# A two-layer diffusion step: feed-forward borders with weight splits behind the first half's tiles, a fixed order of the first seven-product blocks, and the output weights' splits one piece ahead

## The chip, the core and the metric

The kernel runs on one core of a Trainium2 chip. The core has five engines that run their own instruction streams: TensorE (PE, matrix products), VectorE (DVE), ScalarE (ACT), GpSimd (POOL) and SyncE (SP, which here issues nearly all transfers). They wait for each other on semaphores only. The metric is the device time of one execution in microseconds (us).

## The reference

The program is one inference step of a two-layer backbone for 128 prompt tokens and 512 sample tokens, both of width 1024. The kernel treats them together as 640 columns, in two halves of 320. Every layer is a mixer (attention) and a feed-forward part; each part is modulated by shift, scale and gate vectors that come from a conditioning vector. The feed-forward part, to which the change belongs, computes

```
h   = rms_norm(x, norm_ffn) * (1 + scale2) + shift2
g, u = split(h @ w_ffn_in)              # 1024 -> 2 x 2816
x   = x + gate2 * ((silu(g) * u) @ w_ffn_out)   # 2816 -> 1024
```

and `mods = silu(cond) @ w_mod + b_mod` gives the shifts, scales and gates of every layer.

## The kernel before

**Arithmetic.** Products are made from a high and a low part of each fp32 operand: `hi = round(a)`, `lo = a - hi`, and three matmuls of 128 x 128 weights on 320 columns (hi x hi, hi x lo, lo x hi; `mm3`, all at L61 in the trace). For every weight tile there is thus a load from memory (SP), a high part (ACT, a Copy) and a low part (DVE, a subtraction), before TensorE can use it. `unit` makes such a tile (L162 load, L170 high, L171 low).

**Feed-forward, first stage.** The 2816 hidden features are 22 blocks of 128. Blocks 0 and 1 are plain (`eight`): for each of eight input tiles k, three matmuls with the gate weight (`fg`) and three with the up weight (`fu`), for the left half of the columns (`fg_00`) and for the right half (`fg_01`). Blocks 2 to 21 use seven block products in the manner of Strassen (`product`, four tiles each, 12 matmuls): the input operands D, N, C, E and the pairs of `h01q` tiles are sums made once per layer by `add_up`; the weights X, Y, Z, W of each block are made from its raw gate and up weights `wg`, `wu` (class `Weights`): four sums on DVE (`s`, written `s13` and `s24` in the source), then a high part (`hi`, ACT) and a low part (`lo`, DVE) of each. A block's products come as X, D (with weight Y), N (with Z), the second X, Z, C (with Y), and E (with W) one block later. `job` is the block before, whose E product, gate and hidden value are finished during the present one. For blocks 2 and 3 the two X products are made ahead (`ahead`), among the plain blocks. Names: `h01q` are the input tiles of layer 0 (`h11q` in layer 1), `wgu` a plain block's weights, `wX`, `wY`, `wZ`, `wW` the others, `fd` the bank of D and Z, `fg` that of X, N, C and E.

**The border before it.** The first half's norm and the input tiles come out of the mixer's output stage: `oanacc` sums the squares of the eight output tiles (L205 on DVE; `ocnacc` in layer 1), two matmuls with ones (`oanp`) make the second half's row sums while the first tiles of block 0 run, and `make` writes each input tile's high and low part: for the left half, even k on DVE (L293 and L294), odd k on POOL (L290 and L291); for the right half, high on ACT and low on DVE (L287, L288).

**Second stage.** The output product has eight output tiles n and the 22 hidden blocks, taken in two passes: FIRST (9 blocks), SECOND (13 blocks). Hidden blocks that were written to memory (`sp`) are read back as `hr` (function `again`, helper `some`). `wout` loads a piece of the output weights and splits it (`wo_0_45`: pass 0, output tile 4, from block 5 on; L1329 on ACT, L1330 on DVE). Each output bank (`fo_...`) is added to the residual `xr` by DVE (L313).

**Side work.** The modulation of the next part is made on DVE during this: `step` loads weight tiles `wm` and multiplies them with `silu(cond)`, held in `cb` (`junk`, L1418, two operations of 128 x 1024 for each tile). Two Silu operations on ACT prepare `cb` (L1422).

**What sets the order.** The code is written per operation, and a scheduler puts the instructions of each engine in an order from its own costs and the dependences; each engine then runs its list strictly in order. `after(inst, fn)` forces what `fn` issues behind `inst` on the same engine; class `Line` chains the operations of one stream (`dve`, `act`) in the order in which they are written. Buffers rotate: `rawp` holds three raw weight tiles for all loads by `load`, so that a load waits until the third tile before it is used up. SP issues transfers in order, and a transfer that waits holds up those behind it.

## Time and profile before

| what | value |
|---|---|
| time, median of three runs (range) | 1534.39 us (1533.13 to 1541.67) |
| the profiled execution: its time, its span | 1534.34 us, 1532.5 us |
| TensorE busy, share of the span | 1465.5 us, 96% |
| DVE, ACT, POOL busy | 1143.5 us (75%), 738.4 us (48%), 230.2 us (15%) |
| granted TensorE clock | 0.994 |
| layer 0: first matmul of blocks 0 and 1, of block 2, of the output product, of layer 1 | 394.73, 433.36, 674.72, 834.29 us |
| layer 1: first matmul of blocks 0 and 1, of block 2, of the output product | 1083.32, 1121.92, 1364.51 us |

A timeline row has the start in us, the duration, the engine, the line, the operation, what it writes and reads, and in brackets how long the engine sat idle before it and which engine's work ended that wait. A row of windows has the busy time and the number of instructions (x) of an engine in a stretch. The span is what lies between the first and the last instruction; 1.8 us of the time lie around it. A matmul's duration reads longer than the step to the next one, since matmuls overlap.

### The profile page before, as it was taken

What the parts mean: (1) busy time and instruction counts of PE and PEld (TensorE: products, weight loads), DVE (VectorE), ACT (ScalarE), POOL (GpSimd) and SP (SyncE); (2) the same over time, 40 slices, a digit from 0 to 9 for tenths busy, and PEclk for the clock granted to TensorE, in tenths of its full rate; (3) what the DMA queues carried; (4) which work ended last, traced back from release to release, by engine and by line L of the source; (5) the groups of instructions that cost most, each with busy time, mean ns of one, the idle gap of its engine ahead of it and who ended that gap; (6) DMA issues with size and microseconds to landing.
All of it is one profiled execution on the core that took longest, in us unless ns stands there. A gap on an engine that the chain in (4) does not pass through costs nothing.

```text
span 1532.5 us, 25615 instructions
## 1 busy us (share of the span) xinstructions
PE 1465.5 (96%) x9928; PEld 1409.3 (92%) x9928; DVE 1143.5 (75%) x2115; ACT 738.4 (48%) x1447; POOL 230.2 (15%) x303
## 2 busy tenths in 40 slices
PE   5999989989999999999999899999999999999997
PEld 4889878879999999999999889989989999999997
DVE  5646687875889999957998787765888997743333
ACT  5445577763655444431224556663655444441221
POOL 0215635522100000000002433212100000000000
PEclk9999999999999999999999999999999999999999
DMA  9324541005155555578773210003154555367211
GB/s 370 112 95 170 170 141 39 18 21 172 43 189 176 177 180 190 174 261 307 232 227 120 90 41 29 28 15 110 42 190 162 176 181 159 128 233 251 85 41 69
DMA packets 73674, 215.09 MB, mean 140 GB/s; under 512 B 8160, under 2 KB 13040, under 8 KB 73296
## 3 DMA queue, kind: packets, MB, share of 16 engines
q1 hardware_dynamic: 71504, 210.09, 41.3%
q10 hardware_dynamic: 1632, 2.43, 0.5%
q8 instruction: 78, 1.28, 0.3%
q0 software_dynamic: 416, 0.93, 0.2%
q14 instruction: 44, 0.36, 0.1%
HBM read 184.96 MB, written 28.46 MB: 139 GB/s over the span
## 4 chain that ended last, share of the span: by engine, by line
PE 80%; DVE 10%; ACT 5%; DMA 2%; issue 2%; POOL 0%; POOLq 0%; DVEq 0%; SPq 0%; ACTq 0%
PE fg L61 18%; PE fo L61 10%; PE fd L61 9%; PE fu L61 5%; PE gq L61 2%; PE nk L61 2%; PE nq L61 2%; PE go L61 1%; PE fo_4b L61 1%; PE fo_2b L61 1%; PE fo_0b L61 1%; PE fo_0a L61 1%; PE fo_4a L61 1%; PE fo_2a L61 1%; PE fo_6a L61 1%
## 5 line engine op out<-in xcount | busy, mean ns | idle before, releaser
L1078 ACT ACTIVATE sg<-g 128x320 f32<-128x320 f32 x40 | 18.9, 472 | 154.2 <-DVE g L1078 154.2
L1418 DVE SCALAR_TENSOR_TENSOR junk<-wm,cb 128x1024 bf16<-128x1024 f32 x62 | 75.6, 1220 | 3.2 <-DMA wm<-in_wm 2.4
L245 POOL TENSOR_SCALAR h10h<-h10t,gs,mods 128x320 fp32r<-128x320 f32 x4 | 3.6, 892 | 426.4 <-DVE h10t L239 424.7
L61 PE MATMUL gq<-h10h,wgq 128*128 128x320 f32 x256 | 65.6, 315 | 0.2
L1078 DVE SCALAR_TENSOR_TENSOR junk<-wm,cb 128x1024 bf16<-128x1024 f32 x50 | 61.0, 1220 | 0.8
L1078 DVE TENSOR_TENSOR wZ<-s,wZ 128x1024 fp32r<-128x1024 f32 x40 | 48.7, 1218 | 0.8 <-ACT wZ L1078 0.8
L1078 DVE TENSOR_TENSOR wY<-s,wY 128x1024 fp32r<-128x1024 f32 x40 | 48.7, 1218 | 0.0
L61 PEld LDWEIGHTS gq<-h10h,wgq 128*128 128x128 f32 x256 | 44.7, 188 | 1.6 <-PE gtp L65 1.0
L1078 ACT ACTIVATE wY<-s 128x1024 fp32r<-128x1024 f32 x40 | 42.0, 1050 | 7.5 <-DVE s L1078 7.5
L1078 ACT ACTIVATE wZ<-s 128x1024 fp32r<-128x1024 f32 x40 | 42.4, 1061 | 1.5 <-DVE s L1078 1.5
L313 DVE SCALAR_TENSOR_TENSOR xr<-fo,mods,xr 128x320 f32<-128x320 f32 (+2 forms) x48 | 19.6, 435 | 29.8 <-PE fo L61 29.7
L1602 ACT ACTIVATE gp<-gs,gb,rq 128x640 f32<-128x640 f32 (+1 forms) x40 | 31.9, 798 | 19.7 <-DVE gb L1601 17.6
L61 PE MATMUL fg<-h11N,wZ 128*128 128x320 f32 x240 | 39.1, 310 | 1.9 <-ACT wZ L1078 1.2
L61 PE MATMUL fd<-h01D,wY 128*128 128x320 f32 x240 | 39.2, 309 | 1.5 <-ACT wY L1078 1.3
L61 PE MATMUL fd<-h11D,wY 128*128 128x320 f32 x240 | 39.2, 309 | 1.5 <-ACT wY L1078 1.3
L1078 DVE TENSOR_TENSOR sg<-up,sg 128x640 f32<-128x640 f32 (+1 forms) x40 | 31.4, 785 | 12.2 <-ACT sg L1078 12.2
L61 PE MATMUL fg<-h01N,wZ 128*128 128x320 f32 x240 | 38.9, 310 | 0.9 <-ACT wZ L1078 0.9
L61 PE MATMUL gq<-h10l,wgq 128*128 128x320 f32 x128 | 39.4, 308 | 0.0
L61 PE MATMUL fg<-h01q,wX 128*128 128x320 f32 x240 | 38.8, 309 | 0.0
L61 PE MATMUL fg<-h11q,wX 128*128 128x320 f32 x240 | 38.8, 309 | 0.0
L61 PE MATMUL fd<-h01q,wZ 128*128 128x320 f32 x240 | 38.6, 309 | 0.1
L61 PE MATMUL fd<-h11q,wZ 128*128 128x320 f32 x240 | 38.6, 309 | 0.0
(3024 smaller groups left out, 5323.3 us busy)
## 6 DMA issues: line engine op xcount, KB each, us to landing
wm<-in_wm SPq DMA_DIRECT2D x48, 512.0 KB, 3.6
mraw<-in_wm SPq DMA_DIRECT2D x24, 512.0 KB, 3.7
mraw<-in_wm SPq DMA_DIRECT2D x8, 1024.0 KB, 15.3
wm<-in_wm0g SPq DMA_DIRECT2D x8, 512.0 KB, 3.5
x<-in_xT SPq DMA_DIRECT2D x8, 320.0 KB, 5.5
xr<-in_xT SPq DMA_DIRECT2D x8, 320.0 KB, 5.6
cb<-in_crow SPq DMA_DIRECT2D x2, 1024.0 KB, 5.7
gt<-in_rpbp SPq DMA_DIRECT2D x8, 240.0 KB, 3.5
```

The costliest lines, as they stand in the source:

```text
L61: cls.last = nc.tensor.matmul(*a, **k)
L245: G.tensor_scalar(h[:, c0:c1], t, self.gsl[:, k, 0:1], self.ml[:, self.sh + k, 0:1], ALU.mult, ALU.add)
L313: V.scalar_tensor_tensor(xo[:, c0:c1], ps[:, c0 - o:c1 - o], ml[:, g + n, c:c + 1], xi[:, c0:c1], ALU.mult, ALU.add)
L1078: self.last = after(self.last, lambda: op(*a, **k))
L1418: def step(kind, at, line=lambda op, *a, **k: op(*a, **k)):
L1602: S.activation(dst, src, AF.Exp, bias=nb, scale=rq[:, j:j + 1], accum_out=ll[:, j:j + 1])
```

## The change

Three places are edited, in both layers.

**The border to block 0.** Tiles k = 5 and 7 of the left half are made by DVE and no longer by POOL (per layer four POOL operations less, four DVE operations more). The low parts of `wX_3` and of block 1's two weights `wgu_10`, `wgu_11` are forced behind the last tile's low part (`hm.done`; being a DVE instruction, this orders DVE alone). Block 1's raw weights no longer use the rotating `rawp` tiles, but the two tiles named "ws", which are free until the first block's sums; SP issues one of these loads ahead of the `xr` loads and one behind them in layer 0.

On DVE, at the end of the first half's norm, there stood before (`wX_3`, `wgu` low parts; `h01t` is x times the norm's factor; `xr_...` with `oanrs` a tile of the right half from `xr_4359` on):

```order
L205 TENSOR_TENSOR oanacc<-oanacc,oansq_4862 128x320
L171 TENSOR_TENSOR wX_3_5019<-wX_3r,wX_3_5019 128x1024
L293 CAST h01q_4751<-h0132d_4741 128x320
L205 TENSOR_TENSOR oanacc<-oanacc,oansq_4878 128x320
L294 TENSOR_TENSOR h01q_4751<-h0132d_4741,h01q_4751 128x320
L281 TENSOR_TENSOR h01t_4881<-xr_4696,oanrs 128x320
L171 TENSOR_TENSOR wgu_10_5024<-wgu_10r,wgu_10_5024 128x1024
L171 TENSOR_TENSOR wgu_11_5029<-wgu_11r,wgu_11_5029 128x1024
```

and there stands now:

```order
L208 TENSOR_TENSOR oanacc<-oanacc,oansq_4862 128x320
L297 TENSOR_TENSOR h01q_4750<-h0132a,h01q_4750 128x320
L284 TENSOR_TENSOR h01t_4865<-xr_4658,oanrs 128x320
L284 TENSOR_TENSOR h01t_4881<-xr_4696,oanrs 128x320
L208 TENSOR_TENSOR oanacc<-oanacc,oansq_4878 128x320
L296 CAST h01q_4751<-h0132d_4741 128x320
L297 TENSOR_TENSOR h01q_4751<-h0132d_4741,h01q_4751 128x320
L296 CAST h01q_4752<-h0132d_4741 128x320
L297 TENSOR_TENSOR h01q_4752<-h0132d_4741,h01q_4752 128x320
L180 TENSOR_TENSOR wX_3_5019<-wX_3r,wX_3_5019 128x1024
```

The low part of `wX_3` now follows the last sum of squares (`oansq_4878`) and the tiles k = 5 to 7, and the low parts of `wgu` have left this place (they follow nine and eleven rows later).

**The first seven-product blocks.** Block 2's raw weights are fetched and summed earlier, right behind the left half's gate of block 0; its parts are made as X, Y, Z and then W (W was first). For blocks 2 and 3 (`first`), the next block's weight parts are made behind the evacuation of N (`u1`) and not between the products, and every block's D product is forced behind the last matmul that was written before it. The Silu operations on `cb` move two blocks later, into the `act` chain.

On TensorE, at the border to the seven-product blocks, there stood before (the last three matmuls of N of block 2, and what follows; `h01D` and `h01N` are operands, the numbers tell tiles apart):

```order
L61 MATMUL fg_2_4988<-h01N_4772,wZ_2_5305 128x320 x3
L61 MATMUL fd_3_5394<-h01D_4761,wY_3_5326 128x320 x2
L61 MATMUL fg_3_5061<-h01N_4769,wZ_3_5327 128x320
L61 MATMUL fd_3_5394<-h01D_4761,wY_3_5326 128x320
L61 MATMUL fd_3_5394<-h01D_4762,wY_3_5326 128x320
L61 MATMUL fd_2_5314<-h01q_4757,wZ_2_5305 128x320 x3
L61 MATMUL fd_2_5314<-h01q_4758,wZ_2_5305 128x320 x3
L61 MATMUL fd_2_5314<-h01q_4759,wZ_2_5305 128x320 x3
L61 MATMUL fd_2_5314<-h01q_4760,wZ_2_5305 128x320 x3
L61 MATMUL fg_2_4988<-h01C_4765,wY_2_5304 128x320 x3
```

and there stands now:

```order
L61 MATMUL fg_2_4988<-h01N_4772,wZ_2_5046 128x320 x3
L61 MATMUL fd_2_5314<-h01q_4757,wZ_2_5046 128x320 x3
L61 MATMUL fd_2_5314<-h01q_4758,wZ_2_5046 128x320 x3
L61 MATMUL fd_2_5314<-h01q_4759,wZ_2_5046 128x320 x3
L61 MATMUL fd_2_5314<-h01q_4760,wZ_2_5046 128x320 x3
L61 MATMUL fg_2_4988<-h01C_4765,wY_2_5045 128x320 x3
L61 MATMUL fg_2_4988<-h01C_4766,wY_2_5045 128x320 x3
L61 MATMUL fg_2_4988<-h01C_4767,wY_2_5045 128x320 x3
L61 MATMUL fg_2_4988<-h01C_4768,wY_2_5045 128x320 x3
L61 MATMUL fd_3_5392<-h01D_4761,wY_3_5326 128x320 x3
```

Nothing of block 3 (`fd_3`, `fg_3`) stands ahead of block 2's Z and C products any more.

**The output weights.** In the first pass, `prepare(i + 1)` loads and splits the next piece ahead of the present piece's matmuls; the read-backs (`some`) begin with the third output tile. On DVE, around the split of output tile 5's first piece, there stood before:

```order
L313 SCALAR_TENSOR_TENSOR xr_4553<-fo_0_4a,mods_98,xr_4553 128x320
L1418 SCALAR_TENSOR_TENSOR junk_8354,mods_99<-wm_13_8346,cb 128x1024
L313 SCALAR_TENSOR_TENSOR xr_4553<-fo_0_4b,mods_98,xr_4553 128x192
L313 SCALAR_TENSOR_TENSOR xr_4553<-fo_0_4b,mods_98,xr_4553 128x128
L1330 TENSOR_TENSOR wo_0_50_8360<-wo_0_50r,wo_0_50_8360 128x640
L1330 TENSOR_TENSOR wo_0_55_8395<-wo_0_55r,wo_0_55_8395 128x512
```

and there stands now:

```order
L1346 TENSOR_TENSOR wo_0_45_8258<-wo_0_45r,wo_0_45_8258 128x512
L316 SCALAR_TENSOR_TENSOR xr_4419<-fo_0_2a,mods_98,xr_4419 128x320
L1346 TENSOR_TENSOR wo_0_50_8295<-wo_0_50r,wo_0_50_8295 128x640
L316 SCALAR_TENSOR_TENSOR xr_4419<-fo_0_2b,mods_98,xr_4419 128x192
L316 SCALAR_TENSOR_TENSOR xr_4419<-fo_0_2b,mods_98,xr_4419 128x128
L1443 SCALAR_TENSOR_TENSOR junk_8337,mods_99<-wm_12_8333,cb 128x1024
```

`wo_0_50` has moved ahead of the residual of output tile 2 from behind that of tile 4, past three modulation tiles (six `junk` operations); on SP its load moved with it.

The diff, cut to what does this (moved code that is unchanged is left out):

```diff
+    def unit(src, n, name, lo="v", pool=None, behind=None, raw=None):
+        if raw is None:
+            raw = load(src, n, name + "r")
+        else:
+            nc.sync.dma_start(raw, src)
...
-        S.activation(hi, raw, AF.Copy)
-        (V if lo == "v" else G).tensor_tensor(lw, raw, f(hi), ALU.subtract)
+        after(behind, lambda: S.activation(hi, raw, AF.Copy))
+        after(behind, lambda: (V if lo == "v" else G).tensor_tensor(lw, raw, f(hi), ALU.subtract))
...
-            elif k % 2:
+            elif k in (1, 3):
                 G.tensor_scalar(h, h32, 1.0, 0.0, ALU.mult, ALU.add)
                 G.tensor_tensor(l, h32, f(h), ALU.subtract)
             else:
                 V.tensor_copy(h, h32)
-                V.tensor_tensor(l, h32, f(h), ALU.subtract)
+                self.done = V.tensor_tensor(l, h32, f(h), ALU.subtract)
...
+        def fetch_g(fb):
+            if fb == FEW:
+                raws[fb].append(load(wFI[l, fb, 0], 1024, f"wg{l}_{fb}r"))
+            elif fb < FB:
...
+        done = hm.done
...
-        wX += [unit(wFI[l, FEW + i, 1], 1024, f"wX{l}_{FEW + i}") for i in range(1, AHEAD)]
-        w1 = [unit(wFI[l, 1, i], 1024, f"wgu{l}_1{i}") for i in range(2)]
+        wX += [unit(wFI[l, FEW + i, 1], 1024, f"wX{l}_{FEW + i}", behind=done) for i in range(1, AHEAD)]
+        w1 = [unit(wFI[l, 1, i], 1024, f"wgu{l}_1{i}", behind=done, raw=fp.tile([P, 1024], F32, tag="ws", bufs=2, name=f"wgu{l}_1{i}r"))
+              for i in range(2)]
+        fetch_u(FEW)
+        fetch_g(FEW)
+        w = Weights(FEW)
         sg = tmp(f"sg{l}_0")
         gated(sg, 0)
+        w.sums()
...
-        w.hi_w()
-        w.lo_w()
-        w.sums()
         for c in "XYZ":
             w.hi(c)
             w.lo(c)
+        w.hi_w()
+        w.lo_w()
...
+            first = fb < FEW + AHEAD
...
             if n:
                 n.sums()
+            if n and not first:
                 n.hi("X")
...
-            product(b5, w.Y, 0, "D", True)
+            after(PE.last, lambda: product(b5, w.Y, 0, "D", True))
...
             act(S.activation, u1, g[:, :HT], AF.Copy)
             if n:
+                if first:
+                    for c in "XYZ":
+                        n.hi(c)
+                        n.lo(c)
+                    fetch_u(fb + 2)
+                    n.hi_w()
                 n.lo_w()
                 fetch_g(fb + 2)
...
-            step("load", fb + 1)
+            step("load", fb + 1, act)
...
-        for n in range(KT):
-            plan = ((3, 6),) if n < 4 else ((0, 5), (5, 4))
...
+        jobs = [(n, j0, m) for n in range(KT) for j0, m in (((3, 6),) if n < 4 else ((0, 5), (5, 4)))]
+        ready = {}
+        def prepare(i):
+            if i < len(jobs):
+                n, j0, m = jobs[i]
+                ready[i] = wout(j0, m, (n,), f"wo{l}_0_{n}{j0}")[0]
+        prepare(0)
+        for i, (n, j0, m) in enumerate(jobs):
+            prepare(i + 1)
...
+                if n > 1:
+                    some(2)
+                step("n", n)
...
-                    if at == FEW + 1:
+                    if at == FEW + 3:
                         for c in range(2):
-                            S.activation(cb[:, c, :], cb[:, c, :], AF.Silu)
+                            line(S.activation, cb[:, c, :], cb[:, c, :], AF.Silu)
```

More of the change, by code (lines that the diff above doesn't have):

```diff
@@ L1191, in __init__ @@
                 self.u, self.g = raws[fb]
-                self.X = wX[fb - FEW] if fb in early else None
+                self.X = wX[fb - FEW] if fb < FEW + AHEAD else None
             def sums(self):
@@ L1224, in ffn @@
         w = Weights(FEW)
-        w.hi_w()
-        w.lo_w()
+        sg = tmp(f"sg{l}_0")
+        gated(sg, 0)
         w.sums()
+        for k in range(2):
+            hm.add_up(k)
+        for i in range(1, AHEAD):
+            ahead(FEW + i, wX[i])
+        eight(0, w0, 1)
+        for k in range(2, 4):
+            hm.add_up(k)
+        gated(sg, 1)
+        hidden(0, sg)
+        for c in range(2):
+            eight(1, w1, c)
+            if c == 0:
+                sg = tmp(f"sg{l}_1")
+            gated(sg, c)
+        hidden(1, sg)
+        step = side(fk)
+        hd += [[ring.tile([P, T], F32R, tag="hl", name=f"hd{l}_{i}{c}") for c in "hl"] for i in (1, 2)]
         for c in "XYZ":
@@ L1249, in ffn @@
                 act(S.activation, p1, g[:, :HT], AF.Copy)
-            if n:
+            if n and not first:
                 n.hi("Y")
@@ L1255, in ffn @@
                 fetch_u(fb + 2)
-            product(b5, w.Y, 0, "D", True)
+            after(PE.last, lambda: product(b5, w.Y, 0, "D", True))
             act(S.activation, p5, b5[:, :HT], AF.Copy)
-            if n:
+            if n and not first:
                 n.lo("Z")
@@ L1269, in ffn @@
                     dve(V.tensor_tensor, jsg, jup, jsg, ALU.mult)
-            if n:
+            if n and not first:
                 n.hi_w()
@@ L1352, in ffn @@
                     part(pss[n], [w[:, (FIRST.index(blocks[0])) * P:] for w in ws[n]], blocks, c, blocks[0] == FIRST[0], False)
[L1353 to L1355 removed]
+        jobs = [(n, j0, m) for n in range(KT) for j0, m in (((3, 6),) if n < 4 else ((0, 5), (5, 4)))]
[7 more added lines that the diff above has]
+            prepare(i + 1)
+            if n >= 4 and j0 == 0:
                 pss[n] = obank(0, n)
[L1357 to L1358 removed]
+            for c in range(2):
+                part(pss[n], ready[i], FIRST[j0:j0 + m], c, j0 == 0, j0 + m == len(FIRST))
+            if j0 + m == len(FIRST):
                 for c in range(2):
[L1360 to L1364 removed]
+                    residual(x[n], x[n], pss[n][c], mods[l], G2, n, c)
+                if n > 1:
+                    some(2)
+                step("n", n)
         some(len(later))
```

46 lines of the change are left out of this document (8 added, 38 removed).

## The prediction

> **What bounds the kernel now.** I read the page first, the shares of the engines and the chain of work that ended last.
>
> ```profile
> PE 1465.5 (96%) x9928; PEld 1409.3 (92%) x9928; DVE 1143.5 (75%) x2115; ACT 738.4 (48%) x1447; POOL 230.2 (15%) x303
> PE 80%; DVE 10%; ACT 5%; DMA 2%; issue 2%; POOL 0%; POOLq 0%; DVEq 0%; SPq 0%; ACTq 0%
> ```
>
> TensorE sets the end, and the change takes no matmul away. So it can only win TensorE's idle time at the places that it edits. Windows around these places, a steady stretch, and the two borders as a whole size it:
>
> ```profile
> 394.00:412.00 18.00, 15.67 (x104) 14.98 (x103) 15.99 (x32) 13.33 (x30) 3.97 (x4) 1.00 0.25 89
> 430.00:475.00 45.00, 42.56 (x282) 41.14 (x282) 39.60 (x56) 25.82 (x40) 0.00 (x0) 1.00 0.54 182
> 475.00:655.00 180.00, 180.00 (x1230) 180.00 (x1229) 173.24 (x252) 88.92 (x146) 0.00 (x0) 1.00 0.57 181
> 705.00:735.00 30.00, 28.07 (x190) 27.55 (x189) 24.51 (x45) 4.12 (x6) 0.00 (x0) 1.00 0.80 269
> 1084.00:1104.00 20.00, 17.67 (x117) 16.98 (x116) 17.63 (x35) 15.83 (x35) 3.97 (x4) 1.00 0.23 79
> 1120.00:1170.00 50.00, 46.63 (x309) 44.90 (x308) 41.36 (x58) 27.65 (x44) 0.00 (x0) 1.00 0.52 177
> 394.00:475.00 81.00, 76.23 (x507) 74.12 (x506) 73.04 (x128) 51.68 (x99) 3.97 (x4) 1.00 0.41 137
> 1083.00:1164.00 81.00, 75.30 (x499) 72.89 (x498) 71.89 (x126) 51.33 (x98) 3.97 (x4) 1.00 0.40 137
> ```
>
> After the stretch come its length and, for PE, PEld, DVE, ACT and POOL, the busy time and the instructions. In the steady stretch (475 to 655) a matmul takes 180/1230 = 0.1463 us, with no idle time. At that step the others lose: 18 - 104 x 0.1463 = 2.8 us (norm of layer 0), 45 - 41.3 = 3.7 (border to block 2, layer 0), 30 - 27.8 = 2.2 (output weights, layer 0), 20 - 17.1 = 2.9 and 50 - 45.2 = 4.8 (norm and border, layer 1). Together 16.4 us, 1.1% of the time: nothing above that can be won here. The DVE column warns: DVE is busy 173/180 = 96% of the steady stretch too, and over the whole of norm and border it idles only 81 - 73.0 = 8.0 us (394 to 475) and 9.1 us (1083 to 1164). TensorE cannot come through there faster than DVE. The view of TensorE's waits names what ended them:
>
> ```profile
> PE fd L61 <- ACT wY L1078: 2.6, 2, 1.3
> PE fg L61 <- ACT wZ L1078: 2.1, 3, 0.9
> ...
> PE fg L61 <- POOL h01q L291: 1.2, 1, 1.2
> PE fg L61 <- POOL h11q L291: 1.2, 1, 1.2
> PE oanp L61 <- DVE oanacc L205: 1.1, 1, 1.1
> PE ocnp L61 <- DVE ocnacc L205: 1.1, 1, 1.1
> ...
> PE fo_6a L61 <- DVE wo L1330: 1.0, 1, 1.0
> PE fo L61 <- DVE wo L1330: 0.9, 1, 0.9
> ```
>
> Every one of them is a wait that the change touches, twice where it has both layers.
>
> **The norm of the first half.** The timeline there, on ACT, DVE, POOL and TensorE:
>
> ```profile
> 398.52 0.46 ACT L204 ACTIVATE oansq<-xr 128x320 f32<-128x320 f32 x1
> 397.71 1.90 DVE L171 TENSOR_TENSOR wX<-wX_3r,wX 128x1024 fp32r<-128x1024 f32 x1
> 399.52 0.31 DVE L293 CAST h01q<-h0132d 128x320 fp32r<-128x320 f32 x1
> 399.76 0.48 DVE L205 TENSOR_TENSOR oanacc<-oanacc,oansq 128x320 f32<-128x320 f32 x1
> 400.16 0.48 DVE L294 TENSOR_TENSOR h01q<-h0132d,h01q 128x320 fp32r<-128x320 f32 x1
> 400.97 1.21 DVE L171 TENSOR_TENSOR wgu<-wgu_10r,wgu 128x1024 fp32r<-128x1024 f32 x1
> 397.53 0.99 POOL L291 TENSOR_TENSOR h01q<-h0132a,h01q 128x320 fp32r<-128x320 f32 x1
> 402.58 1.70 POOL L291 TENSOR_TENSOR h01q<-h0132d,h01q 128x320 fp32r<-128x320 f32 x1
> 400.29 0.81 PE L61 MATMUL oanp<-oanacc,ones 128*128 128x320 f32 x2 [1.15 <-DVE oanacc L205]
> 404.34 0.57 PE L61 MATMUL fg<-h01q,wgu 128*128 128x320 f32 x2 [1.19 <-POOL h01q L291]
> ```
>
> The last sum `oanacc` has its input at 398.52 + 0.46 = 398.98, but `wX_3` holds DVE until 399.5. Behind it now, `wX_3` no longer delays it. TensorE started 0.53 after that addition did (400.29 - 399.76), so it would start at about 399.5. It arrived at 400.29 - 1.15 = 399.14, and in the new order `oanp` stands three matmuls (0.44) earlier, so it arrives at 398.7. A wait of 0.8 stays, and the two small matmuls themselves cost some 0.2: 1.0 of the 2.8 us stays. The second wait, for tile 7 from POOL, goes: on DVE its two operations (0.31 + 0.48) follow those of tiles 5 and 6, and 399.5 + 2 x 0.8 = 401.1 is before TensorE needs it (404.34 - 1.19 = 403.15, and 0.8 us earlier by the gain on `oanp`). The four added DVE operations, 2 x 0.79 = 1.6 us per layer, are paid from the 1.90 and 1.21 that leave this place. Those lows are needed only by the X products of block 3 and by block 1, seven us or more later, so moving them costs nothing as long as DVE idles at all before that; if it did not, the bound is their own 1.2 us each. Gain 1.8 in layer 0 and 1.9 in layer 1; bounds 0 and 2.8 or 2.9 each.
>
> Were the added operations on DVE to meet POOL, they would be dearer: `wX_3` took 1.90 beside the POOL row at 397.53, and 1.21 is what its like took at 400.97. The Trainium skill, "SBUF — State Buffer", section "SBUF: two separate sides", has DVE and GpSimd share one pair of ports as an exclusive lock, the later one blocked for the whole instruction. By that rule 398.52 - 397.71 = 0.81 us of the 1.90 are blocking, the trace has 0.69, and the POOL move alone would already give this 0.7 us back; the sum above does not depend on it.
>
> **The border to block 2.** Again TensorE, and what it waited for:
>
> ```profile
> 439.03 0.56 PE L61 MATMUL fd<-h01D,wY 128*128 128x320 f32 x2 [1.29 <-ACT wY L1078]
> 440.48 0.42 PE L61 MATMUL fg<-h01N,wZ 128*128 128x320 f32 x1 [0.89 <-ACT wZ L1078]
> 441.03 0.75 PE L61 MATMUL fd<-h01q,wZ 128*128 128x320 f32 x4
> 437.92 1.06 ACT L1078 ACTIVATE wY<-s 128x1024 fp32r<-128x1024 f32 x1 [1.65 <-DVE s L1078]
> 439.26 1.22 DVE L1078 TENSOR_TENSOR wY<-s,wY 128x1024 fp32r<-128x1024 f32 x1
> 441.61 0.68 DVE L1078 TENSOR_TENSOR wW<-wg_3r,wW 128x512 fp32r<-128x512 f32 x1
> 444.75 0.49 DVE L1078 TENSOR_TENSOR g<-fg,p 128x320 f32<-128x320 f32 x1 [1.19 <-PE fg L61]
> ```
>
> The matmuls that wait at 439.03 and 440.48 belong to block 3, whose weights are not ready; the 24 matmuls of block 2 behind them (from 441.03) had their weights already. The order alone costs 2.2 us, twice. In the new order Z and C of block 2 come first, 24 x 0.1463 = 3.5 us of cover. With t the end of block 2's N product, block 3's weights now start behind its evacuation: `u` at t + 0.2, high part of `wY_3` to t + 1.6, low to t + 2.8; needed at t + 3.5. Then on DVE low of `wZ_3` to 3.95, `wW_3` 4.6, `up` 5.0, `g` 5.4; E of block 2 needs that `g`, and stands 37 matmuls behind t, at t + 5.4. So the step that is late next is E, by nothing or some tenths, in both first blocks. Block 2's own weights, which cost the rest of the 3.7, are now loaded and summed while the right half still runs. TensorE reaches this border 1.8 us earlier, and DVE has to follow: its 8.0 us of idle time in layer 0 shrink by the gain and by the 1.6 us of added operations, and grow by the 0.7 that `wX_3` no longer loses beside POOL. With the full 1.8 + 3.7 it would be left 1.6 us of 75, 2%, less than the 4% of the steady stretch. So I let 1.1 us of waits stay here in layer 0 and 1.3 in layer 1: gain 2.6 and 3.5. Bounds: 3.7 and 4.8 above; below, rival 1.
>
> The two Silus on `cb`, each as large as the high part of `wY` (1.06 us), move to where ACT idled 2.79 us (the row below), and the modulation reads `cb` only behind them. That costs nothing; in the old place they were in no wait of TensorE that I count, bound 2.1 us on ACT's chain.
>
> ```profile
> 455.99 0.47 ACT L1078 ACTIVATE sg<-g 128x320 f32<-128x320 f32 x1 [2.79 <-DVE g L1078]
> 350.83 0.55 DVE L313 SCALAR_TENSOR_TENSOR xr<-oa0a,mods,xr 128x320 f32<-128x320 f32 x1 [7.68 <-PE oa0a L61]
> ```
>
> The raw load of `wgu_10` now stands on SP ahead of the eight `xr` loads. The first `xr` user (350.83) had waited for TensorE and not for a load, so this costs nothing, as long as the loads land in time; the 512 KB ahead of them bound it at 1.9 us per layer (estimate, at the 269 GB/s of the stretch from 705 to 735).
>
> **The output weights.** In layer 0:
>
> ```profile
> 714.97 1.22 DVE L1418 SCALAR_TENSOR_TENSOR junk<-wm,cb 128x1024 bf16<-128x1024 f32 x1
> 716.86 0.81 DVE L1330 TENSOR_TENSOR wo<-wo_50r,wo 128x640 fp32r<-128x640 f32 x1
> 717.73 0.41 PE L61 MATMUL fo<-hd_1h,wo 128*128 128x320 f32 x1 [0.92 <-DVE wo L1330]
> ```
>
> `wo_50` was split behind the modulation. In the new order it stands six of these 1.22 us operations earlier, 7 us for a wait of 0.9, and `wo_60` likewise. Gain 2.0 of 2.2. The modulation comes later by the splits that pass it, and the second pass's `wo_1_00` stands behind one `junk` more; DVE idled 30 - 24.5 = 5.5 us between 705 and 735, which covers it; if not, one wait of 1.22 us returns.
>
> **Sum.** 1.8 + 1.9 + 2.6 + 3.5 + 2.0 = 11.8 us. The profiled execution took 1534.34 us (span 1532.5), the median is 1534.39; 1534.3 - 11.8 = **1522.5 us**, 0.8% less.
>
> **The rivals.**
>
> *1. The first blocks hang on DVE.* All of block 3's weights now stand between the evacuation of N and `g`, on one DVE stream. If high and low parts do not overlap, the way from t to `g` is 1.6 + 1.22 + 1.06 + 1.22 + 2 x 0.68 + 2 x 0.49 = 7.4 us against 5.4: 2 us of wait, in two blocks of two layers, 8 us. Speaking for it: DVE's 96%, and nothing may be pulled in front of E any more. Against: high and low parts lie on two engines, so that only the first low part has nothing beside it. From 1 us to 2 us late, 4 to 8 us: 1526 to 1530. Chance 0.18.
>
> *2. The norm's waits stay*, because the sums follow ACT, not `wX_3`, or tile 7 is late on DVE: then 3.7 us are lost of the sum, 1526.2. For it: 0.8 us stay in any case. Chance 0.10.
>
> *3. Slower, by the fixed order.* The same four places, but with DVE stopped in front of block 3's weights: the hidden value's low part (`hd_0l`) must wait for the store of the old one, and the store stands on SP behind the load of `cb`. Each us costs 4, since TensorE has no other matmul to take; from 11.8 / 4 = 3 us late per block it is no gain, and at 5 us, for instance 2 from rival 1 and 3 for a store, 1542. Before, none of TensorE's waits shown names a store or what depends on one. Chance 0.05.
>
> *4. No effect*, if the waits only move to the next late thing: 1532 to 1535, chance 0.05.
>
> **How the numbers follow.** The forecast has 0.62, with its own range of 1518 (all 16.4 us won) to 1526. A measurement can tell about 0.5%, 7.7 us, so faster means below 1526.7: all of the forecast, a fifth of rival 1, more than half of rival 2: 0.62 + 0.04 + 0.06 = 0.72. Slower is rival 3 alone, 0.05; the rest, 0.23, is the same. The range of 1517.5 to 1530 takes in rivals 1 and 2.
>
> **What would show it.** In the profile after: no TensorE wait on POOL in the norm, and one of about 0.8 us on `oanacc`; Z and C of block 2 directly behind N without a wait, and at E of blocks 2 and 3 none over 0.3 us; no wait on `wo`. The window of the steady blocks must lose nothing. I am wrong if the waits at E sum to 4 us, if new waits appear on DVE in the output's second pass, or if the windows shrink and the span does not.

## The result, and the profile after

The changed kernel took 1520.72 us (median; 1519.63 to 1523.6), the kernel before 1536.05 us beside it on the same chip (median of six: five from 1533.13 to 1541.67 us, and one of 3435.48 us, which the ratio leaves out): a ratio of 0.9902, with a 95% interval of 0.9879 to 0.9925. It is faster by about 1%. The prediction was 1522.5 us, 0.8% less, in a range of 1517.5 to 1530. The profiled execution after has a span of 1518.7 us, against 1532.5: 13.8 us won where 11.8 were forecast.

First the page after, its busy shares and its chain of work that ended last:

```profile
PE 1465.9 (97%) x9928; PEld 1412.6 (93%) x9928; DVE 1139.9 (75%) x2123; ACT 738.3 (49%) x1447; POOL 222.4 (15%) x295
PE 82%; DVE 10%; ACT 4%; DMA 2%; issue 2%; POOL 0%; DVEq 0%; SPq 0%; ACTq 0%; POOLq 0%
```

TensorE does the same 9928 matmuls in the same busy time, within 0.4 us. What went is idle time, as the chain also has it (TensorE's share 80% before, 82% now). Where it went is seen from the first matmul of each stage, read from the timelines of both kernels:

| stage (from one first matmul to the next), us | before | after | difference | predicted |
|---|---|---|---|---|
| all before block 0 of layer 0 (not edited, but for the order of loads) | 394.73 | 394.83 | +0.10 | 0 |
| layer 0: blocks 0 and 1, with the norm | 38.63 | 36.59 | -2.04 | -1.8 |
| layer 0: seven-product blocks, with the border | 241.36 | 237.68 | -3.68 | -2.6 |
| layer 0: output product | 159.57 | 157.09 | -2.48 | -2.0 |
| layer 1: mixer (not edited, but for the order of loads) | 249.02 | 249.98 | +0.96 | 0 |
| layer 1: blocks 0 and 1, with the norm | 38.60 | 36.59 | -2.01 | -1.9 |
| layer 1: seven-product blocks, with the border | 242.59 | 238.00 | -4.59 | -3.5 |
| layer 1: output product, to the end | 167.97 | 167.96 | -0.01 | 0 |

The windows after: norm and border of layer 0 (the same 507 matmuls as between 394 and 475 before), of layer 1 (the same 499), a steady stretch, and the output weights. Columns as in the prediction.

```profile
394.10:469.38 75.28, 74.68 (x507) 74.07 (x506) 70.61 (x130) 51.17 (x98) 0.00 (x0) 1.00 0.42 134
1076.00:1150.40 74.40, 73.75 (x499) 72.89 (x498) 69.47 (x127) 50.40 (x96) 0.00 (x0) 1.00 0.41 135
470.00:650.00 180.00, 180.00 (x1230) 180.00 (x1229) 174.04 (x253) 88.67 (x147) 0.00 (x0) 1.00 0.57 181
699.30:729.30 30.00, 30.00 (x207) 30.00 (x206) 24.23 (x48) 3.27 (x5) 0.00 (x0) 1.00 0.89 323
```

The same work takes 81.0 - 75.28 = 5.7 us less in layer 0 and 81.0 - 74.4 = 6.6 us less in layer 1. The steady stretch has 1230 matmuls in 180 us as before. In this window of the output product TensorE no longer idles. Of the eight groups of waits that the prediction quoted, the view of TensorE's waits after has only these two left:

```profile
PE oanp L61 <- DVE oanacc L208: 0.6, 1, 0.6
PE ocnp L61 <- DVE ocnacc L208: 0.6, 1, 0.6
```

The norm of the first half on DVE and TensorE, from the timeline after:

```profile
398.07 0.45 ACT L207 ACTIVATE oansq<-xr 128x320 f32<-128x320 f32 x1
398.87 0.48 DVE L208 TENSOR_TENSOR oanacc<-oanacc,oansq 128x320 f32<-128x320 f32 x1
399.41 0.81 PE L61 MATMUL oanp<-oanacc,ones 128*128 128x320 f32 x2 [0.60 <-DVE oanacc L208]
400.39 0.49 DVE L297 TENSOR_TENSOR h01q<-h0132d,h01q 128x320 fp32r<-128x320 f32 x1
400.81 1.22 DVE L180 TENSOR_TENSOR wX<-wX_3r,wX 128x1024 fp32r<-128x1024 f32 x1
```

The last sum starts 398.87 - 398.52 = 0.35 us behind its input, where it stood 0.78 behind it before (399.76 - 398.98). The low part of tile 7 ends at 400.88, and `wX_3` follows it with 1.22 us where it took 1.90. The border to block 2, on TensorE and DVE:

```profile
434.95 1.92 PE L61 MATMUL fd<-h01q,wZ 128*128 128x320 f32 x12
436.70 1.92 PE L61 MATMUL fg<-h01C,wY 128*128 128x320 f32 x12
438.46 1.93 PE L61 MATMUL fd<-h01D,wY 128*128 128x320 f32 x12
440.23 0.30 PE L61 MATMUL fg<-h01N,wZ 128*128 128x320 f32 x1
440.38 2.03 PE L61 MATMUL fg<-h01E,wW 128*128 128x320 f32 x12
...
435.48 1.05 ACT L1081 ACTIVATE wY<-s 128x1024 fp32r<-128x1024 f32 x1
436.43 1.05 ACT L1081 ACTIVATE wZ<-s 128x1024 fp32r<-128x1024 f32 x1
436.57 1.22 DVE L1081 TENSOR_TENSOR wY<-s,wY 128x1024 fp32r<-128x1024 f32 x1 [1.11 <-ACT wY L1081]
439.85 0.48 DVE L1081 TENSOR_TENSOR g<-fg,p 128x320 f32<-128x320 f32 x1
```

Z starts at t = 434.95, and everything behind it runs without a gap. `g` ends at 440.33, and E starts at 440.38.

### The profile page after: what moved, and what is told of

It reads as the page before. It is cut to its first block, busy times and chain, and to the rows that moved or that the text cites. A ratio compares the mean times of both kernels' runs of the same rounds, so it can differ in the third digit from the quotient of the medians.

```text
span 1518.7 us, 25613 instructions
## 1 busy us (share of the span) xinstructions
PE 1465.9 (97%) x9928; PEld 1412.6 (93%) x9928; DVE 1139.9 (75%) x2123; ACT 738.3 (49%) x1447; POOL 222.4 (15%) x295
## 4 chain that ended last, share of the span: by engine, by line
PE 82%; DVE 10%; ACT 4%; DMA 2%; issue 2%; POOL 0%; DVEq 0%; SPq 0%; ACTq 0%; POOLq 0%
PE fg L61 19%; PE fo L61 10%; PE fd L61 9%; PE fu L61 5%; PE gq L61 2%; PE nq L61 2%; PE nk L61 2%; PE go L61 1%; PE fo_4b L61 1%; PE fo_2b L61 1%; PE fo_6b L61 1%; PE fo_0b L61 1%; PE fo_0a L61 1%; PE fo_4a L61 1%; PE fo_2a L61 1%
## 5 line engine op out<-in xcount | busy, mean ns | idle before, releaser
L61 PE MATMUL fg<-h11E,wW 128*128 128x320 f32 x240 | 38.7, 310 | 0.1
L61 PE MATMUL fu<-h01q,wX 128*128 128x320 f32 x240 | 38.6, 309 | 0.0
L61 PE MATMUL fu<-h11q,wX 128*128 128x320 f32 x240 | 38.6, 309 | 0.0
```

What stands on the lines that cost most here:

```text
L61: cls.last = nc.tensor.matmul(*a, **k)
```

## Experiments

On the chips of the experiments the kernel before took 1537.4 to 1537.8 us, about three more than the 1534.39 shown first, so ratios and stage lengths are compared, not single times. A stage is named by its layer: norm (first matmul of block 0 to that of block 2), border (from there to the first of the output product), output (from there to the mixer). The lengths of all kernels, in us:

| kernel | norm, 0 / 1 | border, 0 / 1 | output, 0 | ratio to before (95%) |
|---|---|---|---|---|
| before | 38.63 / 38.60 | 241.36 / 242.59 | 159.57 | 1 |
| changed | 36.59 / 36.59 | 237.68 / 238.00 | 157.09 | 0.9902 (0.9879 to 0.9925) |
| u_norm | 38.63 / 38.61 | 237.68 / 237.66 | 157.09 | 0.9916 (0.9901 to 0.9931) |
| o_pool | 36.61 / 36.62 | 241.69 / 241.11 | 159.57 | 0.9960 (0.9946 to 0.9974) |
| i_pend5 | 36.01 / 36.01 | 237.66 / 237.66 | 157.09 | 0.9879 (0.9864 to 0.9894) |
| o_place | 38.63 / 38.60 | 238.30 / 239.44 | 159.55 | 0.9943 (0.9924 to 0.9963) |
| o_early | 38.62 / 38.60 | 237.79 / 237.80 | 160.24 | 0.9922 (0.9901 to 0.9943) |
| u_place | 36.60 / 36.62 | 239.59 / 241.65 | 157.09 | 0.9926 (0.9905 to 0.9947) |
| u_both | 36.60 / 36.61 | 239.39 / 240.01 | 157.09 | 0.9911 (0.9890 to 0.9932) |
| u_early | 36.59 / 36.60 | 238.39 / 238.94 | 157.09 | 0.9904 (0.9889 to 0.9919) |
| o_strict | 38.61 / 38.61 | 243.22 / 244.39 | 159.57 | 1.0011 (0.9999 to 1.0022) |
| u_wo | 36.60 / 36.60 | 237.66 / 237.67 | 159.80 | 0.9911 (0.9891 to 0.9931) |
| u_cb | 36.60 / 36.59 | 237.66 / 237.67 | 157.09 | 0.9883 (0.9868 to 0.9897) |

Stages that no kernel of the table edits vary by more than some of these terms: the one before block 0 from 393.9 to 397.5 us, the mixer of layer 1 from 248.7 to 250.4, the output stage of layer 0, where it is as before, from 159.55 to 160.24. So a term of 1 us is read from its own stage, and the totals only say whether the sum holds.

### The norm: undone, done alone, and taken one step further

**u_norm** is the changed kernel with the norm as it was before: tiles 5 and 7 on POOL, and no low part forced behind the last tile.

```diff
-            elif k in (1, 3):
+            elif k % 2:
...
-        wX += [unit(..., behind=done) for i in range(1, AHEAD)]
-        w1 = [unit(..., behind=done, raw=...) for i in range(2)]
+        wX += [unit(...) for i in range(1, AHEAD)]
+        w1 = [unit(..., raw=...) for i in range(2)]
```

> The changed kernel with its norm part undone: tiles 5 and 7 on GpSimd again, the low parts of wX_3 and of block 1's weights free to stand in front of the last sum. My theory, that the three places win independently: the two waits of the first half's norm return, 1.1 us on oanacc and 1.2 us on tile 7 in each layer, the stage from the first matmul of block 0 to that of block 2 goes from 36.6 back to 38.6 us in both layers, the later stages keep what they won, and the time is 1520.7 + 4.0 = 1524.7. The rival, that the border was won only because the norm gives DVE a lead: the stage of blocks 2 to 21 grows too, by 1 to 2 us per layer, and the time is 1527 to 1529.

Its waits of TensorE:

```profile
PE fg L61 <- POOL h01q L294: 1.2, 1, 1.2
...
PE oanp L61 <- DVE oanacc L208: 1.1, 1, 1.1
```

The stage is back at 38.63 and 38.61 us, to 0.01 us what it was before, and the later stages keep all their gains. The norm is worth 2.0 us per layer, by itself.

**o_pool** is the kernel before with only the tiles moved; the weights' low parts are not forced behind anything.

```diff
-            elif k % 2:
+            elif k in (1, 3):
```

> The kernel before, with one edit: tiles 5 and 7 on DVE instead of GpSimd. In this order the last sum of squares also comes ahead of wX_3, and tile 7's low part behind wX_3. My theory: of the 2.0 us that the whole norm part wins per layer, about 1.5 come with this one edit (the wait on oanacc falls from 1.15 to about 0.6, that on tile 7 from 1.2 to 0.3 to 0.7), 1534.4 - 3 = 1531.4. The rival, that only the contention with GpSimd counts: 0.7 us per layer, 1533.

That one line gives the whole 2.0 us per layer. DVE in its timeline:

```profile
397.98 0.48 DVE L205 TENSOR_TENSOR oanacc<-oanacc,oansq 128x320 f32<-128x320 f32 x1
...
398.62 1.22 DVE L171 TENSOR_TENSOR wX<-wX_3r,wX 128x1024 fp32r<-128x1024 f32 x1
```

With tile 5 on DVE, the scheduler puts the last sum of squares ahead of `wX_3` by itself, and `wX_3` takes 1.22 us. So the forced order of the low parts isn't needed for the gain. The prediction let the move alone give back 0.7 us; 2.0 were measured, since the move also changes the order and takes POOL's tile 7 out of TensorE's way. The lock that the Trainium skill states ("SBUF — State Buffer", section "SBUF: two separate sides") gave 0.81 us for `wX_3` itself in the prediction; its row lost 0.68 (1.90 to 1.22), which agrees roughly. Not explained here are o_pool's border stages, which its edit does not touch: 0.33 us longer in layer 0, where the clock fell (last section), and 1.48 us shorter in layer 1.

**i_pend5** is the changed kernel with the two `oanp` matmuls behind five tiles of block 0 instead of three.

```diff
-        eight(0, w0, 0, range(3))
+        eight(0, w0, 0, range(5))
         pend()
-        eight(0, w0, 0, range(3, KT))
+        eight(0, w0, 0, range(5, KT))
```

> The changed kernel, but the two row-sum matmuls of the second half stand two tiles later in the code, which puts them four matmuls later on TensorE. My theory: the wait of 0.6 us on oanacc and ocnacc that is left goes, since TensorE then arrives when the sum is ready, and the second half is no later than now: 1520.7 - 1.2 = 1519.5. The rival, that the second half's tiles are then late for DVE: the wait returns at block 0's second half or at the border, 1520.5 to 1522.

```profile
399.38 0.81 PE L61 MATMUL oanp<-oanacc,ones 128*128 128x320 f32 x2
```

The two matmuls no longer wait, and each norm stage loses another 0.58 us: the 0.6 us that stayed. Later stages do not pay for it, although the second half's row sums come later. At 1519.43 us (span 1517.2) it is the shortest kernel of this study. By total time alone it can't be told from the changed kernel (the intervals overlap); by its two norm stages it can.

### The border: each half of the edit on its own

**o_place** is the kernel before with only the weights of blocks 3 and 4 placed behind the evacuation of N.

```diff
+            first = fb < FEW + AHEAD
             if n:
                 n.sums()
+            if n and not first:
                 n.hi("X")
...
             if n:
+                if first:
+                    for c in "XYZ":
+                        n.hi(c)
+                        n.lo(c)
+                    fetch_u(fb + 2)
+                    n.hi_w()
                 n.lo_w()
```

> The kernel before, with one edit: for the first two seven-product blocks the next block's weights are made behind the evacuation of N. TensorE's order becomes that of the changed kernel (Z and C of block 2 directly behind N) without any forced place, while block 2's own weights and the norm stay as before. My theory, that the order behind N is most of the border's gain: the waits of 1.3 and 0.9 us go, 0.2 us for wY_2 and some 0.3 at E stay, the stage of blocks 2 to 21 falls by about 3 us in layer 0 (241.4 to 238.4) and 3.9 in layer 1, and the time by 7 us against the kernel before on the same chip. The rival, that without the early sums of block 2 DVE is late at E: 1 to 1.5 us per layer.

The border loses 3.06 and 3.15 us. What stays are waits for block 2's own weights: 0.2 us in layer 0; 0.7, 0.2 and 0.2 in layer 1.

**o_early** is the kernel before with the opposite half: block 2's raw weights fetched and summed early, W last, block 1's raw weights in tiles of their own, the Silu operations on `cb` in the `act` chain, but not two blocks later; the weights of blocks 3 and 4 stand between the products as before.

```diff
+        fetch_u(FEW)
+        fetch_g(FEW)
+        w = Weights(FEW)
         sg = tmp(f"sg{l}_0")
         gated(sg, 0)
+        w.sums()
...
-        w.hi_w()
-        w.lo_w()
-        w.sums()
         for c in "XYZ":
             w.hi(c)
             w.lo(c)
+        w.hi_w()
+        w.lo_w()
```

> The kernel before, with one part alone: block 1's raw weights in tiles of their own, and block 2's raw weights fetched and summed early (W last). One D matmul of block 3 still stands in front of block 2's Z. My theory: DVE is done with block 2's sums before block 1 ends, so block 3's weights come 2 us earlier against TensorE, the D matmul in front of Z finds its weight, and the stage falls by about 3 us in layer 0 and 4 in layer 1, almost as much as with the order alone: the two are two ways to the same waits. The rival, that only the order takes the waits away: the wait on wY_3 stays at 1 us or more, and the stage falls by 1 us per layer.

The border loses 3.57 and 4.79 us: the whole gain, without the order of the products. On TensorE and ACT there:

```profile
437.96 0.59 PE L61 MATMUL fd<-h01D,wY 128*128 128x320 f32 x3
438.39 1.92 PE L61 MATMUL fd<-h01q,wZ 128*128 128x320 f32 x12
...
436.55 1.06 ACT L1081 ACTIVATE wZ<-s 128x1024 fp32r<-128x1024 f32 x1 [0.35 <-DVE s L1081]
```

Matmuls of block 3 still stand ahead of block 2's Z, and none waits: with block 2's sums out of the way, block 3's come in time, too. So most of the gain of the border can be had in two ways, and the two do not add up: in layer 0, 3.06 and 3.57 for the halves, 3.68 for both. The early sums, the raw tiles and the chained Silu operations were not tried singly.

**u_place** and **u_both** ask what the placement is for, then. u_place is the changed kernel without it; u_both also leaves out the edge that forces every D product behind the matmul written before it.

```diff
-            first = fb < FEW + AHEAD
+            first = False
...
-            after(PE.last, lambda: product(b5, w.Y, 0, "D", True))
+            product(b5, w.Y, 0, "D", True)
```

(u_place has the first of the two.)

> The changed kernel, but the next block's weights of the first two seven-product blocks are made between the products, as in all other blocks; the forced place of the D product stays. In this order two matmuls of block 3's N stand in front of block 2's Z. My theory: TensorE waits there for the high part of wZ_3, which comes at about 436.4 against 434.95, 1.5 us per layer, as it did in the kernel before: 1520.7 + 3 = 1523.7. The rival, that DVE's stream in front of E is what limits these blocks: weights made earlier relieve it, 1520.2 to 1520.7.

> The changed kernel with the first blocks laid out as every other block again (neither the weights behind the first half's tiles nor the order of their own); early raw tiles, early sums, the norm and wo as changed. Placing a block's weights behind the first half's tiles alone came out 1.9 us of the first layer's border stage better than without it, beside a norm that was won; with the norm as before, early sums alone gave the whole border gain (237.8 us for the stage). So: theory, the order of the border is needed once TensorE comes 2 us earlier: the second column block's weights come in time (early), the third's do not; N of that block waits 1 to 1.5 us for wZ_3 in each layer, stage 239 to 239.6 instead of 237.7, total about 3 us over the changed kernel, and up to 1.7 us more in a layer if the granted clock falls to half behind that wait. Rival: the early sums cover it, no wait above 0.3 us, both stages 237.7 to 237.9, total as the changed kernel; then table and placement are not needed at all.

Both lose 1.7 to 1.9 us in layer 0's border. In layer 1's u_both loses 2.0 and u_place 3.7, of which 1.5 come from a fall of the clock (last section). TensorE and ACT in u_both:

```profile
437.52 0.41 PE L61 MATMUL fg<-h01N,wZ 128*128 128x320 f32 x1 [1.19 <-ACT wZ L1081]
...
436.41 1.06 ACT L1081 ACTIVATE wZ<-s 128x1024 fp32r<-128x1024 f32 x1 [1.00 <-DVE s L1081]
```

Counted from the first matmul of block 2, the high part of `wZ_3` starts 4.06 us later here (436.41 - 432.35), and 2.12 us later in o_early (436.55 - 434.43). The difference is the 2.0 us of the norm: TensorE comes that much sooner, and the weights do not, since they hang on DVE, whose rows there follow each other with no gap above 0.1 us. In the changed kernel the same high part starts later still, 5.00 us (436.43 - 431.43), and nothing waits, because 24 matmuls of block 2 stand ahead of its use. So, with the early sums in place, the placement is worth nothing beside the old norm (o_early against u_norm: 0.1 us per layer) and 1.7 to 2.0 us per layer beside the new one.

**u_early** is the changed kernel with block 2's fetch and sums back behind block 1.

```diff
-        fetch_u(FEW)
-        fetch_g(FEW)
-        w = Weights(FEW)
         sg = tmp(f"sg{l}_0")
         gated(sg, 0)
-        w.sums()
...
+        fetch_u(FEW)
+        fetch_g(FEW)
+        w = Weights(FEW)
+        w.sums()
         for c in "XYZ":
```

> The changed kernel, but block 2's raw weights are fetched and summed behind block 1, as before. My theory: the four sums (2.6 us on DVE) stand in front of wY_2 again, TensorE is now 1.9 us earlier at this border, and it waits about 2 us for wY_2 in each layer: 1524.5. The rival, that DVE has idle time enough to take the sums there: no more than 0.5 us per layer, 1521 to 1521.7.

It loses 0.71 and 0.94 us. The raw loads stay early all the same (`wu_2` is issued at 377.56), and so do two of the four sums; what TensorE waits for is something else:

```profile
435.62 2.03 PE L61 MATMUL fd<-h01q,wZ 128*128 128x320 f32 x12 [0.36 <-ACT p L1081]
...
434.51 0.74 ACT L1123 ACTIVATE hd_0h<-sg 128x640 fp32r<-128x640 f32 x1 [2.73 <-DMA sp_0h<-hd_0h]
...
426.38 0.33 SPq L1115 DMA_DIRECT2D sp_0h<-hd_0h  x1
```

The new hidden value must not overwrite the old one before its store has landed, and that store, issued at 426.38, holds ACT until 434.51; the evacuation `p`, for which Z waits, is queued behind it. Why this store took 8 us is not shown; the changed kernel's, issued at 428.40, held nothing up. So the theory, a wait for `wY_2`, missed, and the run doesn't measure what the early sums are worth beside the new order. The wait is of the kind that the prediction's third rival names, on ACT instead of DVE, at less than 1 us.

**o_strict** is the kernel before with only the edge on D.

```diff
-            product(b5, w.Y, 0, "D", True)
+            after(PE.last, lambda: product(b5, w.Y, 0, "D", True))
```

> The kernel before, with one edit: every block's D product is forced behind the matmuls written before it. The two D matmuls of block 3 no longer stand in front of block 2's Z, but two N matmuls of block 3 still do. My theory: these now wait for the high part of wZ_3, which was at 440.4 when TensorE was free at 437.3, so 3.1 us in place of 1.3 + 0.9: 0.9 us slower per layer, 1536.2. The rival, that the forced order is what won the border: 2.2 us per layer, 1530.

It loses 1.86 and 1.80 us in the border, twice what the theory gave:

```profile
441.69 0.56 PE L61 MATMUL fg<-h01N,wZ 128*128 128x320 f32 x2 [2.74 <-ACT wZ L1078]
442.09 3.34 PE L61 MATMUL fd<-h01q,wZ 128*128 128x320 f32 x12
```

The edge alone moves D back, but two matmuls of N of block 3 stay ahead of block 2's Z, and one wait of 2.74 us takes the place of two. The longer wait is 0.56 us of the loss (2.74 against 1.29 + 0.89); most of it is what follows, 12 Z matmuls in 3.34 us instead of 1.92, at half the clock (last section). No run takes the edge alone out of the changed kernel, so what it does there is not shown.

### The output weights and the Silu operations

**u_wo** is the changed kernel with the output stage as before, **u_cb** with the two Silu operations two blocks earlier.

```diff
-            prepare(i + 1)
...
+                (wt,) = wout(j0, m, (n,), f"wo{l}_0_{n}{j0}")
...
+            some(2)
+            step("n", n)
```

```diff
-                    if at == FEW + 3:
+                    if at == FEW + 1:
```

> The changed kernel with the output weights' part undone. My theory: the waits of 0.9 and 1.0 us on wo return in layer 0, none in layer 1, the stage of the output product in layer 0 goes from 157.1 back to 159.6 us, 1523.2. The rival, that the order of wo matters only for the times of the kernel before: no wait, 1520.7.

> The changed kernel, but with the two Silu operations on cb two blocks earlier again. My theory: ACT idles 2.4 us at that point, TensorE waits for nothing of it, the time is the same to 0.3 us, 1520.7. The rival, that they were part of the border's loss: 1 us per layer, 1522.7.

In u_wo both waits return,

```profile
PE fo_6a L61 <- DVE wo L1346: 1.0, 1, 1.0
PE fo L61 <- DVE wo L1346: 0.9, 1, 0.9
```

and the output stage of layer 0 is 2.71 us longer. u_cb lengthens no stage of the table by more than 0.01 us: beside the new order the Silu operations cost nothing in either place.

## Why the prediction was right, and by how much its terms were off

**What bounds the kernel.** The 16.4 us that the windows gave as the most to be won held: 14.8 were won at the edited places (2.0 + 2.0 + 3.7 + 4.6 + 2.5), and 1.0 was lost in a place that nobody edited.

**The norm** (1.8 + 1.9 predicted, 2.04 + 2.01 measured). The mechanism was right, and a wait of 0.6 us stayed where 0.8 was expected: TensorE started 0.54 us behind the last addition (0.53 before), and this came at 398.87, a little ahead of the 398.98 that was assumed, since its input was there at 398.52. What the prediction didn't see is that moving the tiles was enough: it gave `wX_3`'s delay to the forced order (o_pool).

**The border's critical steps.** The prediction's way from the end of N to E can be laid beside the rows: low part of `wY_3` to t + 2.8 (measured 437.79, t + 2.84), needed at t + 3.5 (438.46, t + 3.51), `g` at t + 5.4 (440.33, t + 5.38), E at t + 5.4 (440.38, t + 5.43). High and low parts overlap, as its first rival denied, and E starts 0.05 us after `g`. In layer 1 the timeline has a store and a gap:

```profile
1116.06 0.83 DVE L1124 TENSOR_TENSOR hd_0l<-sg,hd_0h 128x640 fp32r<-128x640 f32 x1 [1.35 <-DMA sp_0l<-hd_0l]
...
1122.03 2.03 PE L61 MATMUL fg<-h11E,wW 128*128 128x320 f32 x12
```

`hd_0l` waits 1.35 us on DVE for the store, `g` ends at 1121.97, and E starts at 1122.03, 0.23 us behind its turn (the matmul before it starts at 1121.65). In u_cb, where no such wait occurs, E follows that matmul 0.16 us later, directly. The rest of what layer 1's border has over the 237.66 us of other kernels, 0.1 us, lies within the Z product. That is all that came of rivals 1 and 3 together.

**The border's size** (2.6 + 3.5 predicted, 3.68 + 4.59 measured) is the step that failed: "So I let 1.1 us of waits stay here in layer 0 and 1.3 in layer 1". Nothing stayed in layer 0, and some 0.3 us in layer 1. The waits were kept because DVE would be left 1.6 us of idle time of 75. It was left 75.28 - 70.61 = 4.7 us. The prediction had DVE's busy time grow by 1.6 - 0.7 = 0.9 us; for the same 507 matmuls it fell from 73.04 to 70.61. Part of this is in single instructions: rows of before, and then groups of the window after (behind the bar the busy time in us and the mean of one in ns):

```profile
402.10 1.47 DVE L171 TENSOR_TENSOR wgu<-wgu_11r,wgu 128x1024 fp32r<-128x1024 f32 x1
403.49 1.14 DVE L281 TENSOR_TENSOR h01t<-xr,oanrs 128x320 f32<-128x320 f32 x1
```

```profile
L284 DVE TENSOR_TENSOR h01t<-xr,oanrs 128x320 f32<-128x320 f32 x11 | 4.7, 483 | 0.0
L180 DVE TENSOR_TENSOR wgu<-wgu_11r,wgu 128x1024 fp32r<-128x1024 f32 x1 | 1.2, 1220 | 0.0
```

Not only `wX_3` had been longer beside POOL: both of these rows lie beside the POOL row of 402.58 to 404.28, one of the eleven `h01t` with 1.14 us in place of 0.48 (0.66 more) and one `wgu` with 0.25 more. That makes 1.6 us in place of the 0.7. The rest is for the most part no work saved. Added up, the durations in the window fall only from 81.0 to 80.3 us, and block 1's `hd_1l` (0.83 us) lies outside the window after, so that for the same work they hardly changed. Busy time counts rows that overlap once, and the overlaps grew from 8.0 to 9.7 us, since more rows follow each other directly. So the idle time of this column depends on how densely the rows lie, and 1.6 us left in it was no sign that DVE would be late. Of the cause "the order alone costs 2.2 us" the runs show that it was one of two covers: the early sums alone would have removed these waits too (o_early), as long as TensorE does not come sooner.

**The output weights** (2.0 predicted, 2.48 measured): both waits went, and the stretch now holds 207 matmuls in 30 us. The term was the waits alone; the window's own loss, 2.2 us, was nearer.

**What was forecast at nothing.** The Silu operations cost nothing (u_cb), the early load on SP nothing that can be seen (its stage came out 0.10 us longer, but varies by 3.6 us between kernels), the steady blocks lost nothing, and the output's second pass took on no wait. Not foreseen were the 0.96 us that the untouched mixer of layer 1 lost (last section). By terms: 0.35 + 2.17 + 0.48 more than forecast, 0.96 + 0.1 less, which is the 2.0 us between 11.8 and 13.8. That the total came so near is in part luck: the edited places won 3.0 us more than forecast, and stages for which nothing was forecast took 1.1 back.

**The rivals.** The first (E late in every first block) and the second (the norm's waits stay) did not come. The third's wait for a store occurs, and costs 0.2 us here and up to 0.9 in u_early, far from the 3 us per block at which it would decide. The fourth, no effect, is excluded by the interval.

## What to carry to other kernels

When an engine is nearly as busy as the one that sets the end, follow the rows that the next product needs, step by step, before waits are written off as unavoidable: here the steps were right to 0.1 us, and the budget of idle time was not. Gains of two edits at one border can overlap and can also need each other: the placement of the weights, worth 6.2 us alone in the two layers and nothing beside the early sums, was worth 3.7 us again once the norm let TensorE arrive 2 us sooner. After moving a wait's cause, try to move the waiting instruction as well: two matmuls put two tiles later gave another 1.2 us.

## What was not expected of the hardware

The granted clock of TensorE falls to half for about 3.4 us behind some short waits, and not behind others that are as long. In the mixer of layer 1, whose instructions on TensorE, DVE, ACT and POOL are the same in both kernels, three windows on TensorE after the change (busy time, matmuls, granted clock, DMA share, GB/s):

```profile
884.23:887.64 3.41, 2.49 (x19) 1.00 0.00 0
887.64:891.05 3.41, 3.41 (x15) 0.50 0.26 59
891.05:894.46 3.41, 3.41 (x27) 1.00 0.23 95
```

and at the same matmuls before:

```profile
890.09:893.50 3.41, 3.07 (x21) 1.00 0.00 0
893.50:896.91 3.41, 2.83 (x24) 1.00 0.00 0
896.91:900.33 3.42, 3.12 (x23) 1.00 0.49 153
```

In both, two waits stand ahead, of 0.33 and 0.59 us after and of 0.34 and 0.58 before. After the change TensorE reached the end of the second of them 8.10 us sooner than before (886.88 against 894.98) and the end of the slow stretch only 6.53 us sooner (892.69 against 899.22). Of the 1.57 us lost, 0.96 remained at the end of the stage. The length of that stage alone would not show it: in the eight experiments without this drop it is 248.7 to 250.4 us.

The experiments have more of this. These are u_place's two layers and layer 0 of o_pool:

```profile
435.85 0.56 PE L61 MATMUL fg<-h01N,wZ 128*128 128x320 f32 x2 [1.48 <-ACT wZ L1081]
436.25 1.95 PE L61 MATMUL fd<-h01q,wZ 128*128 128x320 f32 x12
...
1118.36 0.56 PE L61 MATMUL fg<-h11N,wZ 128*128 128x320 f32 x2 [1.98 <-ACT wZ L1081]
1118.76 2.73 PE L61 MATMUL fd<-h11q,wZ 128*128 128x320 f32 x12
```

```profile
436.46 0.41 PE L61 MATMUL fg<-h01N,wZ 128*128 128x320 f32 x1 [1.49 <-ACT wZ L1078]
```

u_place kept the full clock behind 1.48 us, and had half the clock behind 1.98. From Z to the first D matmul it is 1123.84 - 1118.76 = 5.08 us in layer 1 and 439.80 - 436.25 = 3.55 in layer 0, so the drop cost 1.5 us. o_pool had half the clock behind 1.49 us, and u_both kept the full clock behind 1.78 us in layer 1. So the length of the wait does not decide it between 0.6 and 2 us.

The traces show what does: when the wait falls. Their records of the granted clock put the drops of one trace a whole number of 3.413 us apart, in all thirteen traces: after the change they start at 208.39, 242.52, 843.27 and 887.64 us, which is 10, 176 and 13 such steps. A drop lasts one step or two (only the last runs on to the end). So a clock period that runs through the whole program, and not the wait, sets when a drop can start. The windows above are cut at these steps. After the change both waits of the mixer (884.48 to 884.82 and 886.29 to 886.88) lie in the step ahead of the drop; before, the border at 893.50 lies between them (892.57 to 892.91 and 894.40 to 894.98). At the border to block 2 it goes, in these runs, by how much of one step TensorE was busy. These are the steps that hold the waits in u_place (layers 0 and 1) and in o_pool:

```profile
433.48:436.89 3.41, 1.93 (x14) 1.00 0.92 336
1116.22:1119.63 3.41, 1.43 (x10) 1.00 0.84 272
```

```profile
433.63:437.04 3.41, 1.75 (x11) 1.00 0.65 233
```

The clock fell in the next step behind 1.43 and 1.75 us of busy time (in o_strict behind 0.67 and 1.37), and did not behind 1.93, nor behind the 2.13 us of u_both, whose wait of 1.78 us is cut in two by a step's end at 1119.70. Busy time in these rows is not the whole measure, since the mixer's drop followed 2.49 us of it, some of it in matmuls of two columns; what exactly is counted stays open.

The Trainium skill, "TensorE: Matmul & The Clock Gate", section "What's actually happening", has a free-running window of 3413 ns in which activity is counted, and half the clock until a window has been busy again. The steps of 3.413 us, the half clock and its length agree with it. The practical rule of the same page (section "Why this matters for your kernels") is to have no idle gap above about 3 us between bursts of matmuls; here gaps of 0.6 to 2.7 us were followed by a drop. A short wait of TensorE therefore costs its own length, and at times some 1.5 us more.
